# An encoder block on one core: row sums by 32x32 transposes, fewer norm sums, another opening and another end

## The chip, the cores and the metric

The kernel runs on one core of one Trainium2 chip. TensorE (PE in the profile) multiplies matrices and writes to PSUM; VectorE (DVE), ScalarE (ACT) and GpSimd (POOL) work element by element; SyncE (SP) only issues transfers, as the scalar queue does in a few places. Each engine takes its instructions in order and waits on semaphores of the others. The metric is the device time of one execution in microseconds, a median of several runs.

## The reference

One encoder block on `x` (1024 positions, 1024 channels), float32 throughout, conditioned by a vector `c`:

```
ada = silu(c) @ w_ada + b_ada                    # 6 x 1024: shift1, scale1, gate1, shift2, scale2, gate2
h   = rmsnorm(x, g_mix) * (1 + scale1) + shift1
qa, ka, va, qb, kb, vb, ga, gb = split(h @ w_in)
oa  = dilated sliding-window attention (8 heads);  ob = 2-D neighbourhood attention (8 heads)
x   = x + gate1 * ((sigmoid(ga) * (oa @ w_branch_dil) + sigmoid(gb) * (ob @ w_branch_na)) @ w_out)
h2  = rmsnorm(x, g_ffn) * (1 + scale2) + shift2
u   = depthwise_conv3(h2 @ w_up)
x   = x + gate2 * ((gelu(u_gate) * u_val) @ w_down)
y   = rmsnorm(x, g_final)
```

Two of its sums run over partitions and are what the change is about: the squares of a norm, summed over the 1024 channels for each position, and `silu(c) @ w_ada`, summed over the 1024 entries of `c`.

## The kernel before

Everything is held transposed: channels on the 128 partitions (8 tiles `m` or `k` of 128 channels), positions along the free axis in two halves of 512 (`hf`). Large products are split into a high and a low part of each operand (`split`, lines 54 to 61: ACT copies the high part, DVE or POOL subtracts the low part) and take three matmuls in place of one (`product`, lines 84 to 86).

The stages, in order of time:

1. *Opening* (lines 430 to 570, up to about 73 us): `x` and the first four chunks of `w_ada` are loaded, SyncE issuing them in the order of the code. `warm` keeps TensorE busy with products of ones while the first norm's squares are added on DVE. `wide_sums` sums them over the partitions, then come root and reciprocal (lines 472 to 475), a broadcast of the result by `bcast` into PSUM, its copy `pbs` on ACT for GpSimd, and a loop over `q` that makes two channel tiles of the normalised, modulated input `h` at a time and starts the first query, key and value products. The second half's norm follows, its squares in two accumulators (`square`, `square_sums`).
2. *Chunks 4 to 9 of* `w_ada` (lines 550 to 625, about 73 to 140 us). A chunk `j` is 512 columns of `w_ada`; its 8 blocks of 128 rows come in four loads of two. `row_pairs` multiplies each block by its column of `silu(c)` and adds on DVE, so that `sums[j]` (128x512) is left, whose 128 partitions must be added. `ada_sums` does this on TensorE: for each of four blocks of 128 columns, a matmul with that block as the weight and a column of ones as the moving operand, which puts the 128 sums on 128 partitions of one column. `ada_bias` adds `b_ada` on DVE. The sums of a chunk are emitted two steps after its last rows. Meanwhile TensorE makes the value tensors (`v_wide`) and a second half of queries and keys. `row_pairs` issues the load of the pair seven further on; a load takes a buffer that an earlier pair has left.
3. *Attention* (`slots`, lines 750 to 1200, about 140 to 640 us): lists of jobs by slot, in which TensorE's products for later query, key and gate tiles are fillers (`fill`). What ACT and DVE do for a filler is put into a queue, `aside(ns, one, two)`: `catch_up` emits the `one` of the next entries as far as a credit of time allows, and the `two` of an entry comes at the next `catch_up`. `k_evict` uses it for keys: the high part is copied on ACT, one head at a time, and the low part (line 385) is subtracted on DVE, followed by copies of both onto the other 64 partitions by SyncE.
4. *Branch products* (lines 1205 to 1250, up to about 743 us): 16 items, a tile and a half each; beside them the last two chunks, 10 and 11, of `w_ada`, one block per item (`row_load`, `row_add`), summed by `ada_sums` at items 7 and 15.
5. *Output product, second norm, up product* (from line 1463, to about 1265 us): `out_tile` adds to `x`, squares, and adds the squares on GpSimd or DVE; the last square of a half has a sum group of its own (`add_sums`). From here on the engines' order is found by the planner of the framework, apart from stretches with an order written out.
6. *Down product and end* (from line 1700): the last norm runs over three blocks of positions (512, 256, 256). A block's squares are added on GpSimd up to tile 5; tiles 6 and 7 have sum groups of their own. The normalised output of a block is written while the next block's products run; that of the last block stands at the end, eight DVE instructions and four stores.

`add_sums` and `ada_sums` in full show what a sum group is:

```
for t in range(n):                                              # add_sums, line 108
    pe.matmul(pcol[:, t:t + 1], sq[:, t * 128:(t + 1) * 128], ones, ...)
for m in range(n):                                              # ada_sums, line 170
    pe.matmul(pa[:, m:m + 1], w[:, m * 128:(m + 1) * 128], col, ...)
```

A float32 matmul appears in the profile as two instructions, so that a group over 512 columns is eight.

## Time and profile before

| | |
|---|---|
| time, median of 3 runs | 1493.36 us (1491.71 to 1493.61) |
| the profiled execution | 1490.45 us, its span 1488.6 us |
| mean granted clock of TensorE | 0.996 |
| busy: PE, DVE, ACT, POOL | 1471.5, 935.8, 773.6, 763.2 us |
| instructions: PE, DVE, ACT, POOL | 7652, 1760, 1442, 635 |
| moved by DMA | 210.29 MB |

A row of the timeline reads: start and duration in us, engine, line of the code, operation, what it writes and reads, shape, count, and in brackets the engine's idle time before it and what ended it. PEld is TensorE's weight load, which overlaps its matmuls. Spans of TensorE's instructions overlap too; the distance from one start to the next is what an instruction holds the engine for. Rows that follow each other and are alike are merged (x8).

### The profile page before, as it was taken

What the parts mean: (1) busy time and instruction counts of PE and PEld (TensorE: products, weight loads), DVE (VectorE), ACT (ScalarE), POOL (GpSimd) and SP (SyncE); (2) the same over time, 40 slices, a digit from 0 to 9 for tenths busy, and PEclk for the clock granted to TensorE, in tenths of its full rate; (3) what the DMA queues carried; (4) which work ended last, traced back from release to release, by engine and by line L of the source; (5) the groups of instructions that cost most, each with busy time, mean ns of one, the idle gap of its engine ahead of it and who ended that gap; (6) DMA issues with size and microseconds to landing.
All of it is one profiled execution on the core that took longest, in us unless ns stands there. A gap on an engine that the chain in (4) does not pass through costs nothing.

```text
span 1488.6 us, 21635 instructions
## 1 busy us (share of the span) xinstructions
PE 1471.5 (99%) x7652; PEld 1252.7 (84%) x7652; DVE 935.8 (63%) x1760; ACT 773.6 (52%) x1442; POOL 763.2 (51%) x635
## 2 busy tenths in 40 slices
PE   9999999999999999999999999999999999999997
PEld 8888888889798998888888778888888888878887
DVE  7783546555555666566515897666666667887865
ACT  5522666666655666653345464444444447485542
POOL 4131332433234354422268668766766676988711
PEclk9999999999999999999999999999999999999998
DMA  9587233445645556577544314222222234542313
GB/s 367 195 303 258 73 97 87 139 108 140 160 148 140 152 156 170 164 259 254 193 152 140 105 43 141 86 85 81 82 70 84 73 133 141 198 141 72 110 36 114
DMA packets 117301, 210.29 MB, mean 141 GB/s; under 512 B 42788, under 2 KB 55716, under 8 KB 117156
## 3 DMA queue, kind: packets, MB, share of 16 engines
q1 hardware_dynamic: 115192, 205.95, 43.2%
q10 hardware_dynamic: 2000, 2.95, 0.5%
q8 instruction: 60, 0.98, 0.3%
q14 instruction: 49, 0.40, 0.1%
HBM read 163.58 MB, written 42.66 MB: 139 GB/s over the span
## 4 chain that ended last, share of the span: by engine, by line
PE 86%; DVE 4%; POOL 3%; DMA 2%; issue 2%; ACT 2%; SPq 0%; DVEq 0%; POOLq 0%; ACTq 0%
PE pj L1326 11%; PE pj L1325 11%; PE pj L1324 11%; PE pj L84 11%; PE pj L86 10%; PE pj L85 10%; PE pj L414 3%; PE O L1027 2%; PE T L1014 1%; PE S L992 1%; PE pv L289 1%; PE pv L291 1%; PE pv L290 1%; PE O L858 1%; PE O L807 1%
## 5 line engine op out<-in xcount | busy, mean ns | idle before, releaser
L61 POOL TENSOR_TENSOR wlo<-wraw,whi 128x512 fp32r<-128x512 f32 (+1 forms) x84 | 106.2, 1287 | 146.1 <-ACT whi L57 145.9
L84 PE MATMUL pj<-h,whi 128*128 128x512 f32 x432 | 178.3, 413 | 0.1
L86 PE MATMUL pj<-h,wlo 128*128 128x512 f32 x432 | 170.0, 394 | 0.0
L85 PE MATMUL pj<-h,whi 128*128 128x512 f32 x432 | 169.6, 392 | 0.0
L1324 PE MATMUL pj<-op,wsh 128*128 128x512 f32 x408 | 159.1, 391 | 1.4 <-ACT op L1254 0.6
L1325 PE MATMUL pj<-op,wsh 128*128 128x512 f32 x408 | 159.0, 390 | 0.9 <-DVE op L1255 0.6
L1326 PE MATMUL pj<-op,wsl 128*128 128x512 f32 x408 | 157.6, 389 | 0.0
L681 DVE TENSOR_TENSOR tl<-T,th 128x512 fp32r<-128x512 f32 (+3 forms) x120 | 77.2, 654 | 106.7 <-ACT th L680 105.4
L731 POOL TENSOR_TENSOR wlo<-wraw,whi 128x512 fp32r<-128x512 f32 x58 | 74.3, 1294 | 125.7 <-ACT whi L730 125.7
L61 POOL TENSOR_TENSOR wsl<-big,wsh 128x512 fp32r<-128x512 f32 (+1 forms) x86 | 111.8, 1323 | 42.5 <-ACT wsh L57 37.6
L673 ACT ACTIVATE P<-P,st 128x256 f32<-128x256 f32 x128 | 64.2, 502 | 93.3 <-DVE st L672 93.3
L1561 DVE SCALAR_TENSOR_TENSOR big<-pj,sm,big 128x512 f32<-128x512 f32 (+2 forms) x183 | 94.9, 563 | 16.5 <-ACT big L1555 15.6
L86 PEld LDWEIGHTS pj<-h,wlo 128*128 128x128 f32 x432 | 81.1, 188 | 18.0
L1324 PEld LDWEIGHTS pj<-op,wsh 128*128 128x128 f32 x408 | 76.6, 188 | 19.3 <-ACT wsh L57 1.5
L1325 PEld LDWEIGHTS pj<-op,wsh 128*128 128x128 f32 x408 | 76.6, 188 | 18.1 <-DVE op L1255 1.2
L84 PEld LDWEIGHTS pj<-h,whi 128*128 128x128 f32 x432 | 81.6, 189 | 11.5 <-issue 0.5
L1325 PE MATMUL pj<-op,whi 128*128 128x512 f32 x232 | 90.4, 390 | 0.0
L1326 PE MATMUL pj<-op,wlo 128*128 128x512 f32 x232 | 90.3, 389 | 0.0
L1324 PE MATMUL pj<-op,whi 128*128 128x512 f32 x232 | 90.2, 390 | 0.0
L85 PEld LDWEIGHTS pj<-h,whi 128*128 128x128 f32 x432 | 81.8, 189 | 10.0
L1326 PEld LDWEIGHTS pj<-op,wsl 128*128 128x128 f32 x408 | 76.6, 188 | 16.0 <-POOL wsl L61 0.3
L61 POOL TENSOR_TENSOR wsl<-wraw,wsh 128x384 fp32r<-128x384 f32 (+1 forms) x46 | 57.3, 1268 | 62.0 <-ACT wsh L57 54.5
(403 smaller groups left out, 4171.7 us busy)
## 6 DMA issues: line engine op xcount, KB each, us to landing
wraw<-w_in SPq DMA_DIRECT2D x32, 512.0 KB
wada<-w_ada SPq DMA_DIRECT2D x31, 512.0 KB
big<-w_up SPq DMA_DIRECT2D x22, 512.0 KB
wraw<-w_up SPq DMA_DIRECT2D x22, 512.0 KB
big<-as SPq DMA_DIRECT2D x22, 512.0 KB
as<-big SPq DMA_DIRECT2D x21, 512.0 KB
gs<-gs SPq DMA_DIRECT2D x32, 256.0 KB
g<-gs SPq DMA_DIRECT2D x16, 512.0 KB
```

The costliest lines, as they stand in the source:

```text
L61: lo_eng.tensor_tensor(lo[:, i:i + step], raw[:, i:i + step], f(hi)[:, i:i + step], OP.subtract)
L84: pe.matmul(psum, whi[:, k0 + k], mhi, start=k == 0, stop=False)
L85: pe.matmul(psum, whi[:, k0 + k], mlo, start=False, stop=False)
L86: pe.matmul(psum, wlo[:, k0 + k], mhi, start=False, stop=k == n - 1)
L414: pe.matmul(p[:, 256 * r:256 * r + 256], ww[:, k], m[:, r], start=k + x + r == 0, stop=k == KT - 1 and x == 2, skip_group_check=True)
L673: act.activation(pp, pp, AF.Exp, bias=mi, scale=-1.0, accum_out=li)
L681: dve.tensor_tensor(tl[:m, :n], pt[:m, :n], f(th)[:m, :n], OP.subtract)
L731: pool.tensor_tensor(lo[:, i:i + n], raw[:, i:i + n], f(hi)[:, i:i + n], OP.subtract)
L1324: pe.matmul(psum, whi[:, k], bhi, start=j < 4 and k == 0, stop=False, skip_group_check=True)
L1325: pe.matmul(psum, whi[:, k], blo, start=False, stop=False, skip_group_check=True)
L1326: pe.matmul(psum, wlo[:, k], bhi, start=False, stop=k == n - 1, skip_group_check=True)
L1561: dve.scalar_tensor_tensor(y[:, dst], src, wt, y[:, dst], OP.mult, OP.add)
```

## The change

- *Chunks 4 to 9.* `fold` transposes the 128x512 sum in blocks of 32x32 on DVE and reduces each block along its rows, which leaves 128x16: a sum over the partitions of each group of 32. All six chunks go into one tile. `fold_bias` then adds the four groups by four matmuls with a 128x32 selection matrix `pick` (made once from the identity) and adds the bias once for all 24 columns. The sum groups and biases of single chunks in the steps are gone, and with them `due`.
- *Chunks 10 and 11* go the same way, one at a time.
- *Norm sums.* The second half's first norm has one accumulator and one sum group; in the first half of the output stage the last square is added on DVE; in the first two blocks at the end tile 6 is added on GpSimd.
- *Opening.* 35 warming products in place of 38; the root is taken by ACT from the sums in PSUM, with 1/D as scale and eps as bias; the split of the first weights comes behind the broadcast's copy; the product of tile 1 with the broadcast comes behind the first bias.
- *Keys.* In the second attention's keys the low part of the second head becomes an entry of its own in the queue.
- *End.* The root is taken by ACT as in the opening. In the last block a second broadcast is made and copied to SBUF; GpSimd multiplies tiles 4 and 5 (scaled by ACT), DVE the other six; the stores are tiles 0 and 1, 2 and 3, 6, 7 from SyncE and 4 and 5 from the scalar queue.

```diff
+    def fold(dst, acc, tmp):
+        dve.transpose(tmp, acc)
+        dve.tensor_reduce(dst, tmp.rearrange("p (c i) -> p c i", i=32), mybir.AxisListType.X, OP.add)
+    def folds_in(tile, n):
+        pick, sums = tile[:, 0:32], tile[:, 32:32 + 16 * n].rearrange("p (j x) -> p j x", j=n)
+        dve.tensor_reduce(pick, idt.rearrange("p (b i) -> p i b", i=32), mybir.AxisListType.X, OP.add)
+        return pick, sums
+    def fold_bias(c0, n, pa, pick, sums):
+        for q in range(4):
+            pe.matmul(pa[32 * q:32 * q + 32, :4 * n], pick, sums.rearrange("p j (m q) -> p (j m) q", q=4)[:, :, q],
+                      start=True, stop=True, skip_group_check=True)
+        ada_bias(c0, pa, 4 * n)
...
             later(750, lambda: one((0,)))
-            later(750, lambda: one((1,)), two)
+            later(750, lambda: one((1,)), lambda: two((0,)))
+            later(400, lambda: None, lambda: two((1,)))
...
-        warm(38, idle, True)
+        warm(35, idle, True)
...
-        ada_rows(wt[0], acc, range(3, 4), 3, 7)
-        dve.tensor_scalar(r, every(pcol), 1.0 / D, EPS, OP.mult, OP.add)
-        act.activation(r, r, AF.Sqrt)
-        ada_rows(wt[0], acc, range(4, 5), 3, 7)
+        ada_rows(wt[0], acc, range(3, 5), 3, 7)
+        act.activation(r, every(pcol), AF.Sqrt, bias=eps, scale=1.0 / D)
         dve.reciprocal(r, r)
-        qk_split(0, (pool, pool))
         pb = bcast(r, ps_n, "pbc")
         wide_sums(pa, wt[0][2], cs[:, 2:3])
         pbs = early.tile([128, 512], FT, name="mt", bufs=3)
         act.activation(pbs, pb, AF.Copy)
+        qk_split(0, (pool, pool))
         ada_rows(wt[0], acc, range(5, 8), 3, 7)
-        for k in range(2):
-            dve.tensor_tensor(x[0][k], x[0][k], pb, OP.mult)
+        dve.tensor_tensor(x[0][0], x[0][0], pb, OP.mult)
...
             piece_bias(q, pa if q > 1 else every(pa))
+            if q == 0:
+                dve.tensor_tensor(x[0][1], x[0][1], pb, OP.mult)
...
-        pcol = square_sums(accs, lambda: v_products(1, (1,), range(8)))
+        v_products(1, (1,), range(8))
+        pcol = ps_n.tile([128, KT], FT, name="pcol")
+        add_sums(pcol, sqa, True, True)
...
+                if i == 3:
+                    fold(folds[1][:, j - 4], sums.pop(j), early.tile([128, 512], FT, name="mt", bufs=3))
...
-            for j in due.pop(n, ()):
-                ada_bias(4 * j, ada_sums([(sums.pop(j), ones)]))
-            due[n + 2] = [j for j in range(4, 10) if done_rows < 4 * j - 12 <= row_ends[n]]
...
-        for j in sum(due.values(), []):
-            ada_bias(4 * j, ada_sums([(sums.pop(j), ones)]))
+        fold_bias(16, 6, ps_s.tile([128, 512], FT, name="pada", bufs=1), *folds)
...
-        if 0 < m < KT - 1:
-            (dve if hf and m > 2 else pool).tensor_tensor(sqa, sqa, sq, OP.add)
+        if 0 < m < KT - 1 or m and hf == 0:
+            (dve if hf and m > 2 or m == KT - 1 else pool).tensor_tensor(sqa, sqa, sq, OP.add)
...
-                elif m < 6:
+                elif m < (7 if cs.start == 0 else 6):
                     pool.tensor_tensor(sqa, sqa, sq, OP.add)
...
-            before = hf, cs, bcast(rstd_of(pcol, n // 128), ps, "pbc", n // 128)[:, :n]
+            act.activation(r, pcol[:, :n // 128], AF.Sqrt, bias=eps, scale=1.0 / D)
+            dve.reciprocal(r, r)
+            before = hf, cs, bcast(r, ps, "pbc", n // 128)[:, :n]
+        bc2 = bcast(r, ps, "pj", 2, 6)[:, :n]
...
+        for m in (4, 5):
+            act.activation(xs[m], xs[m], AF.Copy, scale=g_fin[:, m:m + 1])
+        act.activation(bs, bc2, AF.Copy)
...
+        for i in range(2):
+            pool.tensor_tensor(ys[4][:, i], xs[4 + i], bs, OP.mult)
...
+        for m in (0, 1, 2, 3, 6, 7):
...
+            dve.scalar_tensor_tensor(yy, xs[m], g_fin[:, m:m + 1], bc, OP.mult, OP.mult)
```

71 lines of the change are left out of this document (35 added, 36 removed).

## The prediction

> **What bounds the kernel now.** I read the page first, then the busy time by stretches, then the timelines of the places that the change touches. The span, the engines' busy shares and the chain that ended last:
>
> ```profile
> span 1488.6 us, 21635 instructions
> PE 1471.5 (99%) x7652; PEld 1252.7 (84%) x7652; DVE 935.8 (63%) x1760; ACT 773.6 (52%) x1442; POOL 763.2 (51%) x635
> ...
> PE 86%; DVE 4%; POOL 3%; DMA 2%; issue 2%; ACT 2%; SPq 0%; DVEq 0%; POOLq 0%; ACTq 0%
> ```
>
> TensorE is busy 99% of the span and carries 86% of the chain, so a TensorE instruction taken away is worth its own time unless a wait takes its place. Where it idles is in the stretches (busy time of PE, PEld, DVE, ACT, POOL, then clock and DMA):
>
> ```profile
> 0.00:20.00 20.00, 18.08 (x131) 17.59 (x132) 10.77 (x22) 10.86 (x18) 2.69 (x6) 1.00 0.93 347
> 380.00:400.00 20.00, 17.49 (x92) 14.55 (x92) 11.50 (x32) 12.78 (x32) 3.97 (x4) 0.91 0.53 122
> 790.00:880.00 90.00, 85.85 (x381) 68.69 (x380) 74.33 (x92) 50.19 (x74) 59.55 (x42) 1.00 0.29 91
> 1440.00:1488.60 48.60, 40.93 (x298) 38.48 (x296) 25.08 (x53) 12.37 (x27) 12.13 (x14) 0.92 0.27 93
> ```
>
> In the first 20 us it is idle 1.9 us, around 390 us 2.5 us, between 790 and 880 us 4.2 us, in the last 49 us 7.7 us; together 16.3 of the 1488.6 - 1471.5 = 17.1 us that it idles at all. The terms below are either TensorE work removed from gapless stretches, or a shorter chain in one of these four places.
>
> **The change, part by part.** *Opening.* The timeline of the first 25 us:
>
> ```profile
> 10.67 0.69 DVE L464 TENSOR_TENSOR sq<-sq,mt 128x512 f32<-128x512 f32 x1
> 12.15 1.06 PE L99 MATMUL pcol<-ones,sq 128*128 128x128 f32 x8
> 13.24 0.16 DVE L472 TENSOR_SCALAR rs<-pcol 128x4 f32<-128x4 f32 x1 [1.04 <-PE pcol L99]
> 16.77 1.28 DVE L483 TENSOR_TENSOR ks<-ks,pbc 128x512 f32<-128x512 f32 x2 [0.32 <-ACT mt L480]
> 18.36 0.81 ACT L239 ACTIVATE h<-ks,ada,am 128x512 fp32r<-128x512 f32 x1 [1.62 <-DVE am L305]
> 19.22 0.73 PE L321 MATMUL pj<-h,whi 128*128 128x512 f32 x2 [0.67 <-ACT h L239]
> 22.85 1.30 ACT L57 ACTIVATE vwh<-kl 128x512 fp32r<-128x512 f32 x2 [1.60 <-DMA kl<-w_in]
> 24.70 1.20 PE L331 MATMUL pv<-vwh,h 128*128 128x256 f32 x8
> ```
>
> The vector adds of the norm end at 10.67 + 0.69 = 11.36, but the warming matmuls hold TensorE until 12.15. Three fewer of them are six instructions at (13.21 - 12.15)/8, about 0.11 us with the tail taken off: 0.65 us, so the sums start where their input is ready. The root read straight from the sums drops the 0.16 us step L472; the copy L480 no longer stands behind two weight splits; and of the two products in L483 only one (1.28/2 = 0.64 us) stands ahead of the first bias instead of both. Of these 0.64 I count 0.45, since the bias then waits for TensorE's sums: the first ACT L239 comes 0.65 + 0.45 = 1.1 us earlier, at 17.25, and the 0.67 us that L321 waits for it stay. That gain does not all last: the first value products (24.70) need two splits of a block whose load ends the 1.60 us wait at 22.85 and which end at 22.85 + 1.30 = 24.15. TensorE, arriving 1.1 earlier at 23.6, waits 0.55 for them. I take **-0.5** (ends 0 and -1.1). The weight split put behind the copy is hidden on scalar by the wait for L239, and its low parts on GpSimd, some 0.5 us later, by GpSimd's wait for that same block's load.
>
> *The groups of one-column products.* Each `ada_sums` and each `add_sums` over 512 columns is eight such instructions:
>
> ```profile
> L170 PE MATMUL pada<-ones,sq x48: 164/250/250, 85.9 to 139.4; 128*128 128x1 f32 x48
> ...
> 85.92 0.95 PE L170 MATMUL pada<-ones,sq 128*128 128x1 f32 x8
> 86.73 0.49 PE L84 MATMUL pj<-h,whi 128*128 128x512 f32 x1
> 87.05 0.40 PE L85 MATMUL pj<-h,whi 128*128 128x512 f32 x1
> ```
>
> Eight hold TensorE from 85.92 to 86.73, 0.81 us, and the next product's own spacing is 0.32 us (86.73 to 87.05) instead of 0.23 (97.75 to 97.98, further on): 0.9 us a group. The second norm loses one group, at a place where its one vector add more (0.69) ends before TensorE has finished the products now put ahead of the sums: **-0.9**. The first half of the output stage loses one and puts a vector add in its chain:
>
> ```profile
> 783.20 0.69 DVE L1476 TENSOR_TENSOR wc<-x 128x512 f32<-128x512 f32 x1
> ```
>
> After this square the add costs another 0.69 plus 0.1 of waiting, about what the removed group costs; TensorE has other products meanwhile. **-0.9** (ends -0.9 and +0.7, if the 790 to 880 chain starts later by the add). At the end, the block of 512 columns loses one group of eight and the first block of 256 one of four, 12 instructions at 0.11: **-1.3**; the GpSimd add that replaces them (0.74 at 256 columns, row below) runs while the last tile's product does.
>
> *The folds of chunks 4 to 9.* Removed: six groups, 5.4 us. Added on TensorE: eight products with a 32-column weight. No row has a 32-column weight; the ends are 0 and the 0.9 of the row above. I take 0.5. The Trainium skill, page "TensorE: Matmul & The Clock Gate", section "LDWEIGHTS (loading the stationary operand)": the load time goes with the number of columns, columns/1.2 ns; an estimate from it for eight 32-column loads is 0.2 us, which would make the sum 0.3 us better here and 0.6 in the two late chunks.
>
> Added on vector: six folds, each a 128x512 transpose and a 128x512 reduction. Neither is in the trace. The fastest 128x512 vector row is L565 (0.48), the slowest undisturbed one L567 (1.54/2 = 0.77), so F, one fold, lies between 0.95 and 1.5 us; I take 1.4, near the slow end, since nothing says either runs in the faster form. While GpSimd subtracts, L567 takes 1.69 (5.06/3), which sets 3.3 for a disturbed fold. Vector, GpSimd and TensorE where it matters:
>
> ```profile
> 87.55 1.54 DVE L567 SCALAR_TENSOR_TENSOR sq<-wada,cs,sq 128x512 f32<-128x512 f32 x2 [3.89 <-DMA wada<-w_ada]
> 89.00 0.48 DVE L565 TENSOR_SCALAR sq<-wada,cs 128x512 f32<-128x512 f32 x1
> 89.52 5.06 DVE L567 SCALAR_TENSOR_TENSOR sq<-wada,cs,sq 128x512 f32<-128x512 f32 x3
> 94.57 1.70 DVE L61 TENSOR_TENSOR vwl<-wraw,vwh 128x512 fp32r<-128x512 f32 x1
> 96.20 0.88 DVE L61 TENSOR_TENSOR vwl<-qs,vwh 128x512 fp32r<-128x512 f32 x1
> ...
> 93.99 1.74 POOL L61 TENSOR_TENSOR vwl<-ks,vwh 128x512 fp32r<-128x512 f32 x1
> ...
> 97.75 0.39 PE L289 MATMUL pv<-vwh,h 128*128 128x512 f32 x1
> 97.98 0.39 PE L290 MATMUL pv<-vwl,h 128*128 128x512 f32 x1
> ...
> 122.75 5.52 DVE L567 SCALAR_TENSOR_TENSOR sq<-wada,cs,sq 128x512 f32<-128x512 f32 x6 [10.83 <-DMA wada<-w_ada]
> 133.12 1.54 DVE L567 SCALAR_TENSOR_TENSOR sq<-wada,cs,sq 128x512 f32<-128x512 f32 x2 [0.52 <-DMA wada<-w_ada]
> 138.74 0.95 PE L170 MATMUL pada<-ones,sq 128*128 128x1 f32 x8
> 139.72 0.16 DVE L177 TENSOR_TENSOR ada<-pada,sm 128x4 f32<-128x4 f32 x1 [4.99 <-PE pada L170]
> ```
>
> The fold of chunk 4 falls into the 3.89 us wait for a load, those of 6 and 7 into the 10.83 us wait: nothing. The fold of chunk 5 comes at 89.0, just ahead of the rows and the four splits L61. Part of the delay is won back, because work pushed behind 95.73, where GpSimd's subtracting ends, runs at 0.9 instead of 1.7: some 0.4. The second split ends at 97.08 now, and TensorE asks for it at 97.98, which becomes 97.08 because one group is gone ahead of it. So a wait of F - 0.4 = 1.0 us appears there. The evictions behind the splits, and the SyncE copies and loads queued behind those evictions, move by the same amount, so the last row loads do too. Then the fold of chunk 8 adds F less the 0.52 us wait and less a removed 0.16 us bias, and that of chunk 9 adds F. Vector ends the last row at 134.66 now. TensorE reaches the last sums at 138.74 now, with 4.99 us of vector waiting for it; that slack is what the change spends. New: vector ready at 134.66 + 1.0 + 0.7 + 1.4 = 137.8; TensorE there at 138.74 - 5 x 0.9 + 1.0 = 135.2: a wait of 2.5. In F, both waits are 3F - 0.7 = 3.5. Net **-1.4** (-5.4 + 0.5 + 3.5); ends -3.2 (F 0.95 and free narrow products) and +0.9 (a disturbed fold of chunk 5, 1.9 more, and narrow products at the full 0.9). This is the term that spoils the most: of 5.4 us removed, 1.4 stay. Of the moved waits, the attention's first loads, queued on SyncE behind the last sums, are released at 138.74 + 0.95 = 139.7 now and at about 135.2 + 2.5 + 0.5 = 138.2 then, so they are not later.
>
> Here a rule of the skill bears. The row: L567 with two SBUF inputs goes from 0.77 to 1.69 beside GpSimd. The Trainium skill, page "SBUF — State Buffer", section "Who interferes with whom", says that vector instructions with two SBUF inputs, or in a two-port mode, contend with GpSimd; a fold's instructions have one input, so by that rule the fold of chunk 5 is not disturbed, and the stage gives -1.4; with a fold disturbed like the row it would give +0.5. No run here shows a one-input reduction beside GpSimd.
>
> *The folds of chunks 10 and 11.* Two groups out (1.8), two times eight narrow products in (1.0): **-0.8** (ends -1.8 and 0). The fold's 1.4 us stand on vector ahead of 24 products of one branch pair, 24 x 0.23 = 5.5 us, and are hidden by them.
>
> *The key low parts.* The one stall around 390 us:
>
> ```profile
> 388.86 2.24 DVE L385 SCALAR_TENSOR_TENSOR kl<-pj,ks 64x512 fp32r<-64x512 f32 x2 [0.41 <-ACT ks L381]
> 391.12 0.42 DVE L672 CUSTOM_DVE_ANT_0 P<-S,bias 128x256 f32<-128x256 f32 x1
> ...
> 394.61 0.66 PE L795 MATMUL T<-idt,P 128*128 128x128 f32 x4 [2.51 <-DVE tl L681]
> ```
>
> Two strided L385 subtractions (2.24 us) stand ahead of the softmax step L672, and TensorE waits 2.51 us for what follows it. Apart, the second comes one fill later, behind L672: its 1.1 us leave the chain, and so does a little of scalar's queue, whose next weight split moves one fill later too: **-1.2** (ends -2.5, the whole stall, and 0, if the second one only changes places with the turn's copy). The second half's two copies on SyncE go one fill later as well; what stands behind them there is a load for a later slot. In the seven other such evictions TensorE does not wait.
>
> *The end.* The last block (the GpSimd row shows the price of a 128x256 add):
>
> ```profile
> 1457.95 0.74 POOL L1798 TENSOR_TENSOR wc<-wc 128x256 f32<-128x256 f32 x1 [9.21 <-ACT wc L1794]
> ...
> 1479.50 0.42 ACT L1794 ACTIVATE wc<-x 128x256 f32<-128x256 f32 x1 [1.02 <-DVE x L1790]
> 1479.96 0.60 PE L108 MATMUL pcol<-ones,wc 128*128 128x1 f32 x4 [0.30 <-ACT wc L1794]
> 1480.61 0.16 DVE L113 TENSOR_SCALAR rs<-pcol 128x2 f32<-128x2 f32 x1 [0.42 <-PE pcol L108]
> 1482.10 3.22 DVE L1814 SCALAR_TENSOR_TENSOR wc<-x,sm,pbc 128x256 f32<-128x256 f32 x8 [0.90 <-PE pbc L121]
> ```
>
> The root read from the sums drops L113, 0.16. Then vector does six of eight normalisations, 2 x 3.22/8 = 0.8 us less. The two that GpSimd does: second broadcast 0.3 after the first (estimate: half of the 0.60 of the four sums L108), copy 0.42, two products of 0.74: 0.3 + 0.42 + 1.48 = 2.2 and some 0.2 of handing over, against 6 x 0.40 = 2.4 on vector. They end together, and the store from scalar's queue stands beside the last one of SyncE's: **-1.0** (ends -1.4, with a smaller last store, and 0, if GpSimd is late by 0.8).
>
> **Sum.** -0.5 - 0.9 - 0.9 - 1.3 - 1.4 - 0.8 - 1.2 - 1.0 = -8.0 us. The profiled execution took 1490.45 us with a span of 1488.6; it becomes 1482.4 with 1480.6. Its time lies 2.9 below the median of the three runs, 1493.36, so the forecast for the median is **1485.4**, 0.54% faster.
>
> **Rivals.** *Slow transposes (slower).* The waits grow by 3 us for each us of F, and without them the sum is -11.5. They eat everything from F = (11.5 + 0.7)/3 = 4.1 us, a transpose of some 3.4 us; at F = 6 the time is +5.8, 1499. For it: no row shows the instruction, and it moves data across lanes. Against: every 128x512 vector row, also the disturbed one at 1.69, lies under half of that. 0.08.
> *The middle gives it back (no change).* Between 790 and 880 TensorE waits for a GpSimd, scalar and vector chain. If that chain starts from its loads and not from TensorE, what was won earlier (0.5 + 0.9 + 1.4 + 0.8 + 1.2 + 0.9 = 5.7) is waited away there, and 2.3 stay: 1491. For it: 4.2 us of idle time. Against: the chain's inputs are the output tiles that TensorE makes, and their buffers come free when it does. 0.12.
> *TensorE keeps the folds' gain.* Loads not moved by the vector delay (1.0), a fold of 0.95 (3 x 0.45 = 1.4) and narrow products for nothing (1.5): 3.9 more, 1481.5. For it: 0.52 us is the only load wait behind 122.75 + 5.52, so loads are close to setting the pace, and they may come earlier; against: SyncE issues them behind the evictions. 0.15.
> *The stage loses instead.* The fold of chunk 5 disturbed, the key parts and the tail giving nothing: -8.0 + 1.9 + 1.2 + 1.0 = -3.9, 1489.5. For it: GpSimd is at work when that fold comes (93.99 is its fourth subtraction); against: three independent places. 0.20.
>
> **How the numbers follow.** The forecast, with its terms moving one by one between their ends (1483 to 1488): 0.45. With the two faster rivals, 0.80 for faster by over 0.2% (3.0 us, about what this kernel's three runs, 1491.71 to 1493.61, can tell from no change); the no-change case gives 0.12, the slow transposes 0.08. The range holds the middle 8 in 10: down to 1481.0, where the folds keep their gain, up to 1491.5, which takes in the no-change case and leaves out the slow transposes.
>
> **What would show it.** Right: the group row L170 under `pada` falls from 48 to none behind 80 us; a TensorE gap of about 1 us near 96 us and of 2 to 3 us at the selection product near 133 us; the stall near 390 us at 1.3; the span's tail from the last sums to the last store 1 us shorter; busy time of TensorE down by some 10 us. Wrong: a fold over 3 us; the selection product without a wait; more than 6 us of idle TensorE between 780 and 870 us; a gap at the opening larger than the 0.67 us before L321 now.

## The result, and the profile after

| | before | after |
|---|---|---|
| time, median | 1492.01 us | 1490.9 us (1485.45 to 1494.87) |
| the profiled execution | 1490.45 us, span 1488.6 | 1485.45 us, span 1483.6 |
| busy: PE, DVE, ACT, POOL | 1471.5, 935.8, 773.6, 763.2 us | 1461.9, 948.5, 774.5, 766.1 us |

The ratio of after to before, compared round by round (which is why it isn't quite that of the medians), is 0.9982 with an interval of 0.9971 to 0.9993: 2.7 us faster, where 8.0 were forecast. The forecast of 1485.4 us for the median is 5.5 too low; the time lies in the range of 1481.0 to 1491.5. The two profiled executions differ by 5.0 us; the execution shown here is the fastest of the changed kernel. From the page of after, its busy times and the shares of the chain that ended last:

```profile
PE 1461.9 (99%) x7580; PEld 1241.6 (84%) x7580; DVE 948.5 (64%) x1771; ACT 774.5 (52%) x1445; POOL 766.1 (52%) x640
...
PE 83%; DVE 6%; DMA 6%; POOL 2%; ACT 1%; issue 1%; SPq 1%; DVEq 0%; POOLq 0%; ACTq 0%
```

TensorE's busy time fell by 9.6 us, as announced, but only 5.0 of them came out of the span: its idle time rose from 17.1 to 21.7 us, and the chain now runs through vector for 6% and through transfers for 6% instead of 4% and 2%. The stretches of after (columns as in the prediction), with the one where the folds end added:

```profile
0.00:20.00 20.00, 16.80 (x125) 16.13 (x126) 11.47 (x21) 10.73 (x18) 2.67 (x6) 1.00 0.92 350
130.00:146.00 16.00, 13.19 (x59) 10.41 (x58) 7.63 (x14) 3.77 (x7) 4.51 (x4) 0.89 0.73 214
380.00:400.00 20.00, 17.95 (x103) 14.91 (x103) 11.96 (x31) 14.48 (x36) 5.41 (x4) 1.00 0.49 129
790.00:880.00 90.00, 86.31 (x384) 69.11 (x383) 79.72 (x100) 49.37 (x73) 60.62 (x43) 1.00 0.31 97
1440.00:1483.60 43.60, 36.29 (x271) 34.38 (x269) 21.46 (x46) 12.42 (x27) 14.62 (x17) 0.91 0.28 98
```

The opening idles 3.2 us instead of 1.9; from 130 to 146 us, where TensorE had no gap before, it idles 2.8 us, and the granted clock of that stretch is 0.89.

To place the differences, the starts of the same products are compared (us). "First score" is the first product with a low part of a key; the second score is the 61st of them, which the expectations below call "the 33rd pair".

| kernel | first q/k product | first score | that second score | first branch product | first up product | first of the last 12 sums | span |
|---|---|---|---|---|---|---|---|
| before | 19.22 | 147.51 | 397.91 | 649.68 | 866.87 | 1478.72 | 1488.64 |
| after | 19.41 | 147.79 | 396.68 | 647.64 | 862.65 | 1474.21 | 1483.63 |
| before, once more | 19.27 | 147.40 | 397.73 | 649.35 | 866.63 | 1481.10 | 1490.89 |
| after, once more | 19.29 | 147.35 | 398.83 | 650.22 | 864.99 | 1478.16 | 1487.33 |

Up to the first score nothing is won, where -2.8 was forecast. From score to score after wins 1.5 in one profile and loses 1.15 in the other; from there to the first branch product it wins 0.8 and 0.2, for which the prediction had no term. The late chunks and the output stage, from the first branch product to the first up product, win 2.2 and 2.5. In the down product 0.7 to 0.8 us of the lead go again in both pairs, between 1300 and 1390 us, where TensorE waits in some executions for a late weight copy on scalar, in the kernel before as well as after (1.03 us at 1357.9 in before_again, 1.31 at 1356.8 in after_again). At the last sums of the second pair the kernel before loses 1.7 us of its own, which is explained under the folds.

### The profile page after: what moved, and what is told of

It reads as the page before. It is cut to its first block, busy times and chain, and to the rows that moved or that the text cites. A ratio compares the mean times of both kernels' runs of the same rounds, so it can differ in the third digit from the quotient of the medians.

```text
span 1483.6 us, 21509 instructions
## 1 busy us (share of the span) xinstructions
PE 1461.9 (99%) x7580; PEld 1241.6 (84%) x7580; DVE 948.5 (64%) x1771; ACT 774.5 (52%) x1445; POOL 766.1 (52%) x640
## 4 chain that ended last, share of the span: by engine, by line
PE 83%; DVE 6%; DMA 6%; POOL 2%; ACT 1%; issue 1%; SPq 1%; DVEq 0%; POOLq 0%; ACTq 0%
PE pj L1337 11%; PE pj L1336 11%; PE pj L1335 11%; PE pj L84 11%; PE pj L86 11%; PE pj L85 11%; PE pj L421 2%; PE O L1035 2%; PE T L1022 1%; PE S L1000 1%; DVE sq L577 1%; DMA wraw<-w_down 1%; PE O L866 1%; PE O L815 1%; PE T L803 1%
```

## The experiments

The times are medians; each ratio is to the kernel before, with its interval. Every kernel starts from the changed one except the two with "before" in their name.

**The opening.** Before, the first q/k product started 0.19 us earlier than after, although the sums of the norm start 0.76 us earlier in after (11.39 instead of 12.15). The timeline of after, two places in the opening:

```profile
16.00 2.49 POOL L61 TENSOR_TENSOR wlo<-wraw,whi 128x512 fp32r<-128x512 f32 x2 [15.58 <-ACT whi L57]
...
17.24 0.16 DVE L309 TENSOR_TENSOR ada<-pada,sm 128x4 f32<-128x4 f32 x1 [0.65 <-PE pada L99]
17.44 1.07 DVE L311 SCALAR_TENSOR_TENSOR am<-ada,sm 128x2 f32<-128x2 f32 x1
18.54 0.81 ACT L245 ACTIVATE h<-ks,ada,am 128x512 fp32r<-128x512 f32 x1 [2.10 <-DVE am L311]
...
25.95 5.00 POOL L503 TENSOR_TENSOR ks<-ks,mt 128x512 f32<-128x512 f32 x4
...
27.23 1.27 DVE L311 SCALAR_TENSOR_TENSOR am<-ada,sm 128x2 f32<-128x2 f32 x1
```

L311, a product of 128x2 elements in `piece_bias`, takes 1.07 and 1.27 us while GpSimd subtracts; L309 with one operand in PSUM takes 0.16 a moment earlier. L311 ends near 18.50, GpSimd's second subtraction at 18.49. In the kernel before the same two instructions (its L305) took 0.16 and 0.30 us: the first began at 18.16, after GpSimd's second subtraction had ended (17.89), the second at 27.03, shortly before the end of one (27.31).

*split_first* puts the weight split back where it stood, which changes the place of three scalar instructions and the moment at which GpSimd starts.

```diff
         dve.reciprocal(r, r)
+        qk_split(0, (pool, pool))
         pb = bcast(r, ps_n, "pbc")
...
         act.activation(pbs, pb, AF.Copy)
-        qk_split(0, (pool, pool))
```

> The changed kernel with the weight split put back ahead of the copy; the only difference is the order of three scalar instructions. Theory 1, the small vector product of the modulation factors (two SBUF inputs) cannot run while GpSimd is inside a subtraction: GpSimd's two subtractions run 15.4 to 17.9 us instead of 16.0 to 18.5, the first such product ends at 17.9 instead of 18.5, the first q/k product of TensorE comes at 18.9 instead of 19.4; the second such product, asked 0.5 us earlier at 26.6, passes at the end of a GpSimd product at 27.2 instead of 28.4, and at 31 us TensorE stands 1.0 to 1.2 us earlier than in the changed kernel. Rival 1, the first bias is set by TensorE's own sums and by the vector and scalar chain: the order of the split does nothing, TensorE within 0.2 us at 19 and at 31 us. Median 1489.8 by theory 1, 1490.9 by the rival.

Measured: 1487.26 us, 0.9963 (0.995 to 0.9976). Its timeline:

```profile
17.52 0.34 DVE L311 SCALAR_TENSOR_TENSOR am<-ada,sm 128x2 f32<-128x2 f32 x1
...
18.77 0.73 PE L327 MATMUL pj<-h,whi 128*128 128x512 f32 x2 [0.77 <-ACT h L245]
...
136.60 0.28 PE L192 MATMUL pada<-mt 128*32 128x24 f32 x8 [2.79 <-DVE mt L182]
137.84 0.40 PE L296 MATMUL pv<-vwl,h 128*128 128x512 f32 x1
138.07 0.39 PE L297 MATMUL pv<-vwh,h 128*128 128x512 f32 x1
```

GpSimd's two subtractions lie at 15.35 to 17.85 here, and the first L311 ends as they end: 0.34 us. The product starts 0.64 us earlier, the second one 1.10. The median fell by more than the 1.1 us that were expected; in the profile half rate stays away at 137 us as well, to which the folds come back.

*one_input* leaves GpSimd where it is and takes the second SBUF operand away from L311: `b_ada` plus one is made beforehand, and two one-column instructions read the sum from PSUM.

```diff
-        dve.scalar_tensor_tensor(am1[:, ks], cc[0][:, 1], 1.0, g_mix[:, ks], OP.add, OP.mult)
+        for i in range(2):
+            k = slice(2 * q + i, 2 * q + i + 1)
+            dve.tensor_scalar(am1[:, k], pa[:, 2 + i:3 + i], b_one[:, k], g_mix[:, k], OP.add, OP.mult)
...
+        pool.tensor_scalar(b_one, b_ada[:, 8:16], 1.0, None, OP.add)
```

> The changed kernel with the modulation factors made by two vector instructions of one column, each with one tensor input out of PSUM and two per-partition scalars, instead of one instruction with two SBUF inputs; GpSimd adds 1 to the bias ahead of them. Nothing else moves. Theory 1 (a two-input vector instruction waits for GpSimd's running instruction): each of the new instructions takes 0.2 us or less at both places, the first bias on scalar starts at 17.7 to 17.9 instead of 18.54, the first q/k product at 18.6 to 18.8 instead of 19.41, the second bias at 26.8 instead of 28.59, and TensorE stands 1.5 to 1.8 us earlier at 31 us. Rival 1b, any small vector instruction waits there, whatever its inputs (for GpSimd's port or for the write): they take 0.5 to 1.2 us as now, and nothing is won. Median 1489.3 by theory 1, 1490.9 by the rival.

Measured: 1489.07 us, 0.9971 (0.9959 to 0.9983). Its timeline at the same two places:

```profile
16.01 2.51 POOL L61 TENSOR_TENSOR wlo<-wraw,whi 128x512 fp32r<-128x512 f32 x2 [6.76 <-ACT whi L57]
...
17.33 0.46 DVE L313 TENSOR_SCALAR am<-pada,bo,sm 128x1 f32<-128x1 f32 x2
...
18.51 0.73 PE L329 MATMUL pj<-h,whi 128*128 128x512 f32 x2 [0.40 <-ACT h L246]
...
25.99 5.04 POOL L506 TENSOR_TENSOR ks<-ks,mt 128x512 f32<-128x512 f32 x4
...
26.48 0.45 DVE L313 TENSOR_SCALAR am<-pada,bo,sm 128x1 f32<-128x1 f32 x2
```

With GpSimd at work at the same times, two instructions take 0.46 us together. The first product starts 0.90 us before that of after, the second 1.27, and at 46 us TensorE is 1.45 ahead of after, 0.3 ahead of before. The cause of the opening's loss is the two SBUF operands of L311 beside GpSimd, and it is shown by taking them away.

**The folds.** In the lines of after, vector, 80 to 140 us (count, then busy time and the mean ns of one), and in its timeline where their results are used:

```profile
L181 DVE STREAM_TRANSPOSE mt<-sq 128x512 f32<-128x512 f32 x6 | 4.3, 712 | 0.2
L182 DVE TENSOR_REDUCE mt<-mt 128x16 f32<-128x512 f32 x6 | 4.1, 686 | 0.2
```

```profile
98.01 0.47 PE L296 MATMUL pv<-vwl,h 128*128 128x512 f32 x1 [0.61 <-DVE vwl L61]
...
137.59 0.28 PE L192 MATMUL pada<-mt 128*32 128x24 f32 x8 [2.81 <-DVE mt L182]
137.79 0.64 PE L295 MATMUL pv<-vwh,h 128*128 128x512 f32 x1
138.23 0.63 PE L296 MATMUL pv<-vwl,h 128*128 128x512 f32 x1
```

The fold takes 1.40 us, the eight narrow products hold TensorE from 137.59 to 137.79, the waits are 0.61 and 2.81 us. The fold of chunk 5 (89.57 to 91.01 us) runs beside GpSimd from start to end and takes no longer than the others. But behind the second wait the products start 0.43 to 0.44 us apart instead of 0.23: TensorE runs at half rate for 8 products and loses 1.7 us more.

Half rate does not follow every such wait. In all 18 traces, up to the last sums, the granted clock is either 1.00 or 0.50, and a stretch of 0.50 lasts 3.41 us or twice that. All switches of the clock in a trace lie on one grid of 3.41 us, which lies differently against the work in each execution. Two neighbouring intervals of this grid, in after and then in split_first (stretch, then busy time of PE, PEld, DVE, ACT and POOL, clock, DMA):

```profile
134.58:137.99 3.41, 0.60 (x10) 0.36 (x10) 2.91 (x5) 0.73 (x2) 0.72 (x1) 1.00 0.34 127
137.99:141.41 3.42, 3.42 (x9) 2.65 (x9) 0.36 (x3) 0.81 (x2) 0.28 (x1) 0.50 0.94 208
```

```profile
132.24:135.65 3.41, 1.57 (x7) 0.95 (x6) 3.27 (x5) 1.79 (x3) 0.00 (x0) 1.00 0.72 250
135.65:139.06 3.41, 2.46 (x18) 2.03 (x19) 1.36 (x5) 0.56 (x1) 1.00 (x1) 1.00 0.64 139
```

In after the wait lies within one interval (2.81 us idle of 3.41), and the next is at half rate. In split_first an edge cuts the wait of 2.79 us into 1.84 and 0.95, and the rate stays full. Among the intervals at full rate between 20 and 1472 us of the 18 traces, all 26 with 2.0 us of idle TensorE or more are followed by half rate; of some 7,500 with 1.7 us or less two are; the six between 1.82 and 1.91 went both ways. Where no half rate followed, the folds did win what was forecast: from 65 us to the first score split_first gains 1.4 us on the kernel before, and two kernels further down, vb_apart and vb_key, 1.8 and 1.7.

The two exceptions are in before_again and before_vb, near the end, where one-column sums of 16 and 8 instructions stand close together. In before_again:

```profile
1453.15:1456.57 3.42, 3.42 (x32) 3.42 (x32) 0.00 (x0) 1.75 (x2) 0.00 (x0) 1.00 0.02 5
1456.57:1459.98 3.41, 3.41 (x18) 3.41 (x18) 1.20 (x4) 1.04 (x3) 0.44 (x1) 0.50 0.01 2
```

TensorE is busy throughout, yet half rate follows; some 2.1 us of the first interval are one-column sums, in before_vb as well. That these count like idle time is an inference from two cases. It cost the kernel before 1.7 us in before_again; in the changed kernel the first of the two groups has 8 instructions, and none of the profiles with its end shows it.

*fold_last* puts the selection products behind all 48 value products, so that TensorE has work while vector ends the last fold; the folds get a tile of their own.

```diff
-        folds = folds_in(early.tile([128, 512], FT, name="mt", bufs=3), 6)
+        folds = folds_in(work.tile([128, 128], FT, name="fold", bufs=1), 6)
...
+        p_next = {st: v_wide(st) for _, st in v_steps[10:]}
         fold_bias(16, 6, ps_s.tile([128, 512], FT, name="pada", bufs=1), *folds)
...
-        v_out(br, st, *v_wide(st))
+        v_out(br, st, *p_next[st])
```

> The changed kernel with the selection products of chunks 4 to 9 behind all 48 value products that follow, instead of behind 18 of them (their input in a tile of its own, so that the other buffers still come free). Theory 2, the 2.8 us wait of TensorE at 134.8 and the 8 products at half rate behind it (8 x 0.2 = 1.7 us) are both the price of the place: no wait, products at 0.227 us throughout, TensorE 4.5 us earlier at the first attention scores; median 1486.4. Rival 2, the gain is waited away at the start of attention, because its loads are released by vector's last fold at 137.5 us in both: a new TensorE wait of over 2 us between 140 and 175 us and a total within 2 us of the changed kernel. Rival 2b, the half rate is not the wait's doing: the wait goes, but some products behind 137 us still run at 0.43 us; 2.8 us won.

Measured: 1484.52 us, 0.9946 (0.9927 to 0.9964). Its timeline at the fold, at the first score and at the key parts:

```profile
141.33 0.39 PE L297 MATMUL pv<-vwh,h 128*128 128x512 f32 x1
141.65 0.28 PE L192 MATMUL pada<-fold 128*32 128x24 f32 x8
...
143.46 0.28 PE L792 MATMUL S<-kl,qs 128*128 128x256 f32 x1
...
389.33 0.69 DVE L941 TENSOR_TENSOR u<-u,fb 128x512 f32<-128x512 f32 x1 [3.82 <-DMA fb<-fcs]
...
391.17 0.50 PE L84 MATMUL pj<-h,whi 128*128 128x512 f32 x1 [4.13 <-DVE kl L391]
```

Wait and half rate are gone, and the first score starts at 143.46, 4.3 us earlier than after. By 391 us 2.6 of that is lost to a longer wait at the key parts (4.13 us instead of 1.52). So the wait at the selection product with the half rate behind it cost 4.3 to 4.5 us, which is what the folds had won; and a gain made here does not pass the place near 391 us whole.

*sums_kept* leaves the folds of chunks 4 to 9 out and puts the groups of one-column products back (the code of `ada_sums` and `due` as before), with all else changed.

```diff
-                if i == 3:
-                    fold(folds[1][:, j - 4], sums.pop(j), ...)
...
+            for j in due.pop(n, ()):
+                ada_bias(4 * j, ada_sums([(sums.pop(j), ones)]))
```

> The changed kernel with chunks 4 to 9 summed as before, by six groups of one-column products; the folds, the transposes and the selection products of these chunks are left out. By the prediction's step the folds win 1.4 us: TensorE 1.4 us later here at the first attention scores (near 146 us) than in the changed kernel. By the traces (wait 2.8 and half rate 1.7 behind it, where 2.5 and nothing were foreseen) they win nothing: TensorE within 0.4 us of the changed kernel there, full rate behind the last sums, and the same median within 1 us.

Measured: 1489.17 us, 0.9979 (0.9963 to 0.9994). Its opening happened to be undisturbed, 0.98 us ahead of after at 28.5 us; at 170 us it is 1.06 ahead. So with the half rate behind their wait the folds win nothing: the predicted -1.4 is 0.

**The key low parts.** Near 391 us both low parts now stand as single instructions, but vector has something else between them. Timeline of after:

```profile
365.56 12.86 SPq L435 DMA_DIRECT2D v<-vbc  x16
...
383.03 1.12 SPq L935 DMA_DIRECT2D fb<-fcs  x2
...
388.13 1.06 DVE L391 SCALAR_TENSOR_TENSOR kl<-pj,ks 64x512 fp32r<-64x512 f32 x1 [0.43 <-ACT ks L387]
...
391.05 0.69 DVE L941 TENSOR_TENSOR u<-u,fb 128x512 f32<-128x512 f32 x1 [1.18 <-DMA fb<-fcs]
391.77 1.08 DVE L391 SCALAR_TENSOR_TENSOR kl<-pj,ks 64x512 fp32r<-64x512 f32 x1
392.91 0.50 PE L84 MATMUL pj<-h,whi 128*128 128x512 f32 x1 [1.52 <-DVE kl L391]
```

L941, the weighing of a pair's output (`weigh`), waits for the load `fb`; the second L391 stands behind it on vector, and TensorE behind that. The load reads factors that SyncE has to store first. They are ready at 376.3, but SyncE, in its order, issues 16 copies of value chunks until 378.4 (`vb_chunks`, 12.86 us); the stores follow from 379.10 and the load at 383.03, and the weighing begins 8.0 us after that.

*after_again* and *before_again* are the two kernels unchanged, to see what varies by itself.

> The kernel before, unchanged, timed against itself. The two profiled executions differ by 5.0 us (1490.45 and 1485.45, both at a mean granted clock of 0.996), the paired medians by 2.7 (ratio 0.9982). Theory A, the clock is drawn by each execution whatever the kernel: this kernel's executions spread over the same clocks as the changed kernel's (0.993 to 0.997), about 1490 us at 0.996 and 1494 at 0.993, and the ratio to itself is 1.000 within 0.001. Theory B, the changed kernel draws the lower clock more often than the kernel before: here most executions stand at 0.995 or above, and a fit at equal clock gives the changed kernel the 5 us of the profiled pair.

> The changed kernel, unchanged, for a second profile. Its mean granted clock over 16 executions was 0.9942, that of the kernel before 0.9966 over 28, and its times fall into 1485 to 1488 us and 1490 to 1495 us. In the first profile TensorE waited 1.7 us near 392.9 us; in the two kernels with other edits of the opening or the folds that drew 4.2 and 4.3 us there, the wait was followed by products at half rate. Theory 3, the changed kernel itself has both cases, and the longer one is the usual one: the profile shows a wait of about 4.2 us near 393 to 394 us with the vector add of the weighted outputs standing ahead of the second key low part and waiting for its load, and a time of 1490 us or more. Rival, the second case belongs to the edits of those kernels alone: 1.7 us again.

Measured: before 1491.65 us, 0.999 (0.9979 to 1.0002); after 1491.07, 0.9975 (0.9962 to 0.9988). The mean granted clock is 0.9966 over 28 executions of the kernel before and 0.9942 over 16 of the changed one (0.9944 over the 10 of after_again): it has more half rate, and not by chance of the first runs. In after_again TensorE waits 2.84 us at the key parts instead of 1.52, and 6.83 us of half rate follow.

*key_undone* puts both low parts back into one entry.

```diff
-            later(750, lambda: one((1,)), lambda: two((0,)))
-            later(400, lambda: None, lambda: two((1,)))
+            later(750, lambda: one((1,)), two)
```

> The changed kernel with the key low parts as before: both in one step, one fill earlier. Theory 3: both stand ahead of the weighing again, TensorE's wait near 394 us is the 2.7 us of the kernel before with some products at half rate behind it, and never 4.3; the median is that of the changed kernel or up to 1.5 us faster (1489.4 to 1490.9), since the edit's 1.2 us are only won where the load comes early. By the prediction's step: 1.2 us slower than the changed kernel, 1492.1.

Measured: 1490.22 us, 0.998 (0.9964 to 0.9995). From first to second score it takes 251.91 us, between the 248.89 and 251.48 of the changed kernel's two profiles; TensorE waits 3.63 us until 395.63, with the weighing behind both low parts and a softmax step, waiting 2.43 us for its load there. No verdict: the place varies by more than the edit is worth.

*weigh_later* was to move the weighing behind the second low part, but it moved that of another pair, near 440 us.

```diff
-                at(s0 + 24 + 2 * n, "last", self.weigh, g, z)
+                at(s0 + 24 + 2 * n + (pr == 3 and n == 0), "last", self.weigh, g, z)
```

> The changed kernel with one vector instruction moved: the first weighing of the last dilated pair, which waits for a load issued on SyncE, stands eight vector instructions later, behind the second key low part instead of ahead of it. Theory 3, the moved low part made TensorE wait for that load: TensorE's wait near 392.9 us (1.7 to 4.3) falls to 0.5 us or less, no half rate behind it, mean granted clock up to 0.996 or more, and the median falls by 3 to 4 us to about 1487.3. Rival 3, the low part is late of its own (scalar's copy ends at 388.1 and vector's softmax steps stand ahead): the wait stays above 1.5 us and the median within 1 us of the changed kernel.

Measured: 1489.66 us, 0.9968 (0.9955 to 0.9981). Near 391 it is the changed kernel again, so it says nothing on the theory; it shows how far the wait goes by itself: the weighing waits 4.19 us for its load and TensorE 4.55 us behind it.

*weigh2* moves the right one, the weighings of the third pair.

```diff
-                at(s0 + 24 + 2 * n, "last", self.weigh, g, z)
+                at(s0 + ((26, 27, 29, 30) if pr == 2 else (24, 26, 28, 30))[n], "last", self.weigh, g, z)
```

> The changed kernel with the first two weighings of the third dilated pair, the ones near 391 and 398 us, two slots and one slot later on vector, behind the second key low part; the load is issued as before. Theory 3b, the order on vector makes the late load TensorE's wait: the second key low part runs at about 390 us, TensorE's wait near 393 us falls under 0.5 us, no half rate behind it; median 3 to 4 us down, to about 1487.3. Rival, what stands behind the weighing waits all the same, only later: a TensorE wait of over 1.5 us between 395 and 405 us.

Measured: 1490.97 us, 0.9983 (0.9966 to 1.0001). Its timeline:

```profile
389.59 1.10 DVE L391 SCALAR_TENSOR_TENSOR kl<-pj,ks 64x512 fp32r<-64x512 f32 x1
...
417.89 0.69 DVE L941 TENSOR_TENSOR u<-u,fb 128x512 f32<-128x512 f32 x1 [8.08 <-DMA fb<-fcs]
...
419.11 0.33 PE L866 MATMUL O<-tl,vv 128*128 128x128 f32 x1 [2.81 <-DVE tl L689]
```

The second low part no longer waits, and the wait near 393 falls to 1.02 us. From score to score it takes 249.2 us, 1.2 less than before, which is what was forecast for the key parts; but this is one profile, and one of the changed kernel has 248.9 with the weighing in front. And the weighing frees `fb` for the next load, which is issued later now: the next weighing waits 8.08 us and TensorE 2.81, with half rate behind it. The wait moved, and the 3 to 4 us expected of the median did not come.

*vb_early* asks for the 16 copies six slots earlier.

```diff
-    at(52, "first", vb_chunks)
+    at(46, "first", vb_chunks)
```

> The changed kernel with the 16 copies of the neighbourhood values (issued on SyncE from 365.5 to 379 us, in front of the factor stores) asked for six slots earlier, where SyncE idles; order on the other queues unchanged. The first edit that was to show this, one weighing moved, moved the weighing of the last pair (near 440 us) and left the one near 391 us where it stood, so it told nothing. In all traces so far the factors are ready at 376.1 (changed kernel) and the load that the weighing waits for lands 7.5 to 8 us after SyncE issues it; SyncE issues it 3 us late in the first profile and 5 us late in the others, behind the copies. Theory 3a, the copies make it late: issued at about 380, it lands at 388; TensorE's wait near 393 us (1.7 to 4.7 in the profiles so far) falls under 0.5 us, no half rate behind it, mean granted clock 0.996; the median falls by 3 to 4 us to 1487.3 and the spread gets narrower. Rival, the load is late of the copies' transfers or of its own latency, or the earlier copies delay weight loads: the wait stays over 1.5 us.

Measured: 1489.2 us, 0.9976 (0.9963 to 0.999). Instead of one long wait there are waits of 0.74 and 0.34 at 377, 0.62 at 385, 1.08, 0.49 and 0.54 between 395 and 400 us, none followed by half rate there; the stretch from score to score takes 252.1 us, no less. The load is issued at 383.64, no earlier than in after: the stores ahead of it now wait for the factors themselves, which are made some 4 us later. So the copies alone do not make the load late. In this kernel the copies do not wait for the last dilated heads, whose values they overwrite, so it does not compute the block, and only its time counts here.

*vb_apart* issues the copies from scalar's queue, one in every third slot, into a scratch of their own; *vb_key* has the key low parts as before beside that, and *before_vb* is the kernel before with the same copies.

```diff
-    at(52, "first", vb_chunks)
+    for n in range(16): at(4 + 3 * n, "last", vb_chunks, *divmod(n, 4))
...
-                sp.dma_start(
+                act.dma_start(
```

> The changed kernel with the 16 copies of the neighbourhood values taken off SyncE: they go from scalar's DMA queue, one in every third slot of attention from the fourth on, into a scratch of their own. (The version that only moved them six slots ahead read values of the last dilated heads that the copies had overwritten, so its output was not the reference's; its time stands.) Theory 3a: the factor stores follow the factors at once, at 376 instead of 379 to 382 us, the load of the weighing lands at 388 or earlier in every execution, TensorE's wait near 393 us falls under 0.5 us with no half rate behind it, the stretch from the first score to the 33rd pair takes 247 to 248 us, and the median falls by 3 to 4 us against the changed kernel, to about 1487, with a narrower spread. Rival: scalar pays for the copies (16 x 0.5 to 0.8 us), or the load is late for another reason: the stretch stays at 250 us or more.

> The version with the copies off SyncE, and the key low parts as before. If the key edit is worth what the prediction said where the load is in time: a wait of 2.5 us near 391 us again and the stretch 1.2 to 2.5 us longer than in that version. If the low parts were never the cause of the old wait: the same stretch within 0.3 us.

> The kernel before with the 16 copies off SyncE in the same way. Against the same edit on the changed kernel it gives the whole change without that queue. By theory 3a the kernel before hardly gains (its low parts stand ahead of the weighing; its wait of 2.7 us near 394 us is their own): 0 to 1 us, and the change is then worth 5 to 6 us (the 5.0 of the first profiled pair, and up to 1 us more), not 2.7. Rival: it gains as much as the changed kernel did, and the change stays worth 2 to 3 us.

Measured: 1500.63 us, 1.0047 (1.003 to 1.0063); 1502.26, 1.0055 (1.0039 to 1.0071); 1507.18, 1.0084 (1.0065 to 1.0103). All three are slower than their parents, for a reason of their own, which the timeline of vb_apart shows ahead of the place in question:

```profile
330.83 0.63 ACT L737 ACTIVATE whi<-wraw 128x512 fp32r<-128x512 f32 x1 [7.84 <-DMA ks<-ks]
...
332.73 1.12 PE L802 MATMUL T<-idt,P 128*128 128x128 f32 x4 [6.28 <-DVE tl L688]
...
400.81 0.68 DVE L940 TENSOR_TENSOR u<-u,fb 128x512 f32<-128x512 f32 x1
...
402.67 0.50 PE L84 MATMUL pj<-h,whi 128*128 128x512 f32 x1 [0.29 <-DVE kl L391]
```

and that of vb_key:

```profile
406.47 1.12 PE L801 MATMUL T<-idt,P 128*128 128x128 f32 x4 [2.48 <-DVE tl L687]
```

Scalar stood still for 7.84 us behind a transfer, until one of the copies was issued from its queue, and TensorE for 6.28; near 257 us the same happened with 4.18 and 3.29. This is the rival's price of the copies on scalar, larger than it said, and the expected medians were missed by some 13 us. At the key parts, though, the load is in time now and the weighing does not wait: TensorE waits 0.29 us with the low parts apart and 2.48, with half rate behind it, with them together. From score to score this is 262.04 against 263.97 us: 1.9 us for the edit where its load is early, in one profile of each; the medians differ by 1.6 us, and their intervals overlap. The whole change is worth 1507.18 - 1500.63 = 6.5 us in this pair, but that does not confirm the theory's 5 to 6: the profile of before_vb has 23.9 us of half rate ahead of the last sums and that of vb_apart 10.2, and the difference alone is worth 6.8 us. That a late load takes the key edit's gain is seen in the rows of each profile; how much it takes rests on weigh2 and on vb_apart against vb_key, one profile each; a load on another queue than SyncE's, without the copies moved, was not tried.

**Together.** *best* is one_input, fold_last and weigh_later, with the first two of the last eight stores issued by SyncE at once.

```diff
-            if m > 5:
+            if m > 5 or m < 2:
                 sp.dma_start(dst[m], yy)
```

> The changed kernel with four edits: modulation factors out of PSUM by one-input instructions, selection products behind all value products, the weighing behind the second key low part, and the first two rows of the end stored one by one. Sum of what the theories give: opening 1.5, folds 4.5, key parts 3.0 to 4.0 (1.7 against the first profile, more against executions with the longer wait), end 0.4: a median of 1481.5 (1480.5 to 1483), with no TensorE wait over 1.5 us between 130 and 400 us. For the end alone: its stores (1 MB in all) leave from 0.4 us earlier on and end 0.4 us earlier if their transfer sets the end, and not at all if the last row's own latency does. Rival, the SyncE queue takes the gain: waits between 320 and 400 us, and under 6 us won.

Measured: 1485.43 us, 0.9938 (0.9925 to 0.995): faster than before by 0.62%, and faster than the changed kernel, but 3.9 over the forecast. TensorE waits 4.04 us at the key parts, with 6.83 us of half rate: the weighing that weigh_later moves is not the one that stands there. *best2* has vb_early for weigh_later, *best3* the copies of vb_apart:

> The changed kernel with modulation factors by one-input instructions, selection products behind all value products, the 16 copies six slots earlier, and the first two rows of the end stored one by one. With theory 3a the 6.3 us that the first three edits had won by 146 us (traces) outlast 400 us and the wait there goes as well: TensorE 8 us earlier than in the changed kernel's first profile at 400 us, median 1481 (1479.5 to 1483), 11 us under the kernel before. Rival, SyncE's queue stays behind: a wait of over 2 us near 390 us, 1485 as in the version before it.

> The edits that won, together: modulation factors by one-input instructions, selection products behind all value products, the 16 copies off SyncE, the first two rows of the end stored one by one. By theory 3a the 6.3 us won by 146 us last: first score at 141.5 us, the stretch behind it 247 to 248 us, span 1476 to 1478 us, median 1479 to 1481. Rival: another transfer of SyncE's takes the place of the copies: the stretch at 251 us or more, as in the version without that edit, median 1484 to 1485.

Measured: 1484.65 us, 0.9948 (0.9928 to 0.9968); and 1494.57, 1.0005 (0.9992 to 1.0017). Both missed their forecast. The first cannot be told from best by its interval, and like vb_early it does not compute the block; the second carries vb_apart's loss. Of the kernels that compute the block, best and fold_last (1484.52) are the fastest, and their intervals overlap.

## Why the prediction was wrong in size, point by point

*Opening: forecast -0.5, measured +1.1.* The step that failed is the chain from the broadcast to the first bias, which held every instruction between them at its price of before. Before, the small product L311 (L305 there) came after a subtraction of GpSimd or at the end of one; 0.7 us earlier it meets one in its middle. The rule that I weighed for the folds (the Trainium skill, "SBUF — State Buffer", section "Who interferes with whom": two SBUF inputs on vector contend with GpSimd) bears on L311 by its words, and the trace agrees: 1.07 us for 128x2 elements, and 0.46 for the two instructions of the form with one input in PSUM. I asked only large instructions for it. The price is not the instruction's size but what is left of GpSimd's. It depends on the phase: of ten profiles of kernels with the changed opening, eight met it so. Without the contention the opening is worth -0.1 (weigh2, at 31 us) to -0.3 (one_input, at 46 us), so the 0.5 was too much besides.

*Second norm: -0.9, measured -0.9* (the distance of the two traces goes from +1.13 to +0.24 at 53 us). Right.

*Folds of chunks 4 to 9: -1.4, measured 0.* The fold's 1.40 us, its indifference to GpSimd, and the waits (0.61 for 1.0; 2.81 for 2.5) were right; the narrow products cost 0.2 instead of 0.5, as the estimate from the page of the Trainium skill had it. The step that failed is the price of the wait: I counted its length and not the half rate behind it, 1.7 us. Where the half rate stayed away, the term came out: 1.4 us in split_first; and with the wait filled (fold_last) the folds win 4.2. My own rows showed it: in the stretch of 380 to 400 us the granted clock is 0.91 where before waits 2.51 us, and I read only the idle time from that line. The page "TensorE: Matmul & The Clock Gate" of the Trainium skill, section "The HAM clock gate", describes it: half rate, 427 ns a product of 512 instead of 216, after an idle window of some 3.4 us. The trace agrees in the rate (0.43 and 0.23 us) but the wait is shorter than 3.4 us, and here 2.0 us of idle time in an interval were enough.

*Folds of chunks 10 and 11, output stage: -1.7, measured -2.2 and -2.5* between the first branch product and the first up product. Right for the two late chunks (-0.9 and -0.7 in the two pairs, -0.8 forecast), where the narrow products are again cheap, 0.25 us busy for all eight; the output stage gives more than its -0.9 (-1.3 and -1.8).

*Key low parts: -1.2, measured about +1.1* (from score to score 250.4 before; 251.4 in the mean of seven profiles with the parts apart, 248.9 to 253.2). The step that failed is "the second comes one fill later, behind L672": one fill later it also comes behind a weighing, which waits for a load. I followed what the instruction left and not what it would stand behind. Where the low part did not stand behind a waiting load, the edit won 1.2 us (weigh2, against before) and 1.9 us (vb_apart, against vb_key), in one profile each; the size of this step is less sure than that of the other two. That the place grows worse the earlier TensorE comes (fold_last: 2.6 of 4.3 us lost) is what my sum had no term for; I had asked the question of 790 to 880 us, where nothing was lost (the distance is -2.4 at 694 us and -4.5 at 871).

*End.* The sums: -1.3, measured -1.3 in the first pair, between 1444 us and the last product (in the second -1.1, with the 1.7 us of half rate in before_again taken off). What the sum had no term for is the 0.7 us lost ahead of them. The tail: -1.0, measured 0: from the last product to the end 10.05 and 9.92 us before, 10.20 and 9.95 after. In after the tail reads:

```profile
1470.97 3.18 POOL L1810 TENSOR_TENSOR wc<-wc 128x256 f32<-128x256 f32 x4 [2.16 <-ACT wc L1806]
...
1474.21 1.50 PE L108 MATMUL pcol<-ones,wc 128*128 128x1 f32 x12 [0.50 <-POOL wc L1810]
...
1476.35 1.09 PE L121 MATMUL pbc<-idt,rs 128*128 128x128 f32 x4 [0.64 <-DVE rs L1822]
```

From the last reciprocal to the end 7.42 us pass, 7.43 before, though vector is done 0.8 us sooner, as forecast. The transfers' view of before, 1481 to 1488.6 us in 40 slices, that of after, 1476 to 1483.6, and that of best, 1476 to 1483.3:

```profile
GB/s 151 345 280 16 0 0 0 0 0 0 0 0 0 0 0 189 356 345 307 264 340 345 291 361 350 350 307 340 356 350 356 291 22 0 0 0 0 0 0 0
```

```profile
GB/s 307 318 33 0 0 0 0 0 0 0 0 0 0 0 0 199 350 345 302 291 345 350 307 356 345 345 345 345 345 345 345 254 5 0 0 0 0 0 0 0
```

```profile
GB/s 320 309 39 0 0 0 0 0 0 0 0 22 303 320 157 348 270 17 45 337 337 331 342 359 331 343 348 353 348 337 331 169 0 0 0 0 0 0 0 0
```

From its first store on the output leaves at about 340 GB/s without a gap, before as well as after: about 1 MB in 3.2 us. By these views the stores set the end, not the last normalisation; I had ended the chain with vector's last instruction. In best the first stores start some 0.8 us sooner, but there a gap follows, and from the last reciprocal to the end 7.09 us pass, against 7.17 and 7.18 in fold_last and after_again. An order that keeps the early stores going was not tried. Beside that, TensorE waits 0.50 us for GpSimd's adds before its last 12 sums; before, eight of them ran while the last tile was still being made, and four remained.

The deviations add up: +2.9 until the first score and -0.6 in the late chunks and the output stage (means of the two pairs), +2.3 at the key parts (by the seven profiles), -0.5 between there and the first branch product, +1.5 behind the first up product (the first pair). This is 5.6 in all, so -8.0 becomes -2.4; the measured ratio says -2.7. The agreement is rough, since each place is known from a few profiles. None of the rivals was it as told. "The stage loses instead" comes near in time (1489.5) and has two of its three places right, the key parts and the tail, for other reasons; its disturbed fold did not happen.

Why the changed kernel's mean granted clock is lower can be read from the profiles: one interval of 3.41 us at half rate takes 0.0011 off the mean, and the difference of 0.0024 is two of them. After_again has one at 137 us and two at 393, the kernel before one at 395. What stays open: why the stretch from the second score to the first branch product is 0.2 to 0.8 us shorter, and how far the load at the key parts could come earlier.

## What to carry to other kernels

When a chain is shortened, look at what every moved instruction arrives beside and behind: a two-element vector product can wait out GpSimd's whole running instruction, and an instruction that is put off by one step can land behind a neighbour that waits for a load. Price a TensorE wait of some 2 us or more with what may follow it, and put work of TensorE's own, already due, into the wait before anything else; here that was worth 4.3 us at the place. Ahead of the end, ask whether the last stores are limited by their start or by their bytes.
